# Four experts instead of two kept on chip at the end of a routed mixture of experts

## The chip, the cores and the metric

The kernel runs on one core of a Trainium2 chip. Five engines work side by side, each on its own list of instructions in order: PE (TensorE, matmul), DVE (VectorE), ACT (ScalarE), POOL (GpSimd) and SP (SyncE, which here only issues transfers). They wait for each other by semaphores. The metric is the time of one execution on the device in microseconds, as the median of several runs. All arithmetic is float32.

## What is computed

One hybrid decoder layer over 1024 tokens of width 1024: sparse attention beside a gated MLP, then a mixture of 32 experts, of which each token uses two, then a norm. The change touches the experts and what stands behind them:

```python
eid = g_idx * EXPERTS_PER_GROUP + e_idx
comb = jnp.sum(jax.nn.one_hot(eid, N_EXPERTS, dtype=jnp.float32) * e_w[..., None], axis=1).astype(h.dtype)
y = jnp.zeros_like(h)
for e in range(N_EXPERTS):
    he = jax.nn.silu(h @ w_gate[e]) * (h @ w_up[e])
    y = y + comb[:, e:e + 1] * (he @ w_down[e])
return y
...
x = x + y.reshape(B, T, D)
return rms_norm(x, final_norm_g)
```

`w_gate` and `w_up` are 1024x256 for each expert, `w_down` is 256x1024: 3 MB per expert, 100 MB in all.

## The kernel before

**Places.** The first six of the 32 places in the program take experts 0 to 5. A run sorts the others by how many tokens chose them, and each further place takes the expert of a certain rank (`ranks`). Behind the first six most odd places (`SMALLS`) are *small*: at most 64 tokens, up to 64 rows of a tile. Places 20, 24 and 28 (`PAIRS`) hold the fullest experts: such a place is two units, a first one of 128 rows (20a) and a second of up to 64 rows (20b) with the same weights. There are 35 units.

**A unit.** POOL gathers the rows of its tokens from DRAM (L1470), PE turns them (`xt`, L1486 or L1497), and PE multiplies by gate and up weights (`gu`). For a unit of 64 rows ACT puts the product aside (`junk`, L1543), PE turns it (`gut`, L1546), and ACT and DVE form silu(gate) x up (`kb`). PE then multiplies by the down weights (`y`), ACT evicts the result to `y` (L1513 for a small, L1591 for others), times each token's weight, and POOL adds its rows into the DRAM tensor `acc` with an indirect transfer (`scatter`, L1603). `acc` holds the layer's `x` to begin with. Two scatters could hit the same row, so each waits until the one before has landed. The results lie in a ring of three pages: an eviction waits until the scatter three before it has landed.

**Weights.** SP issues them in the order of `sequence`, into pages from a common pool, ahead of their use. A small uses them as float32 (one matmul counts as two passes). For the others ACT (`wh`, L132) and DVE (`wl`, L140) split each piece in two parts, and three matmuls (L145 to L147) take the place of one. With `EARLIER = 1` the gate and up weights of place 31 come ahead of the down weights of 29.

**The last two places**, 30 and 31, are small but are not scattered: their weighted results stay in `yh` and `yl` (high and low part, 64 rows each, `down` with `keep`; split weights). `spread` makes `S`, a table of zeros and ones that says to which token each kept row belongs.

**The end** (`finish`): SP reads `acc` back as eight tiles `xf` of 128 tokens (L1759). For each tile PE places the kept rows by `S` (four matmuls into `fin`, L1793); DVE adds `xf` (or PE does so for tiles 4 and 6, by a product with the identity, L1791). Square, root and reciprocal follow, the product with `final_norm_g` (`fg`, loaded by POOL at L1755), and the store (L1774). Four small lists (`lst`, `lsr`, `lsw`, `eod`) go to DRAM for a loop over overflow blocks that these inputs do not enter.

The order in each engine's list is set by a scheduler that places instructions by an estimate of times; `issue_after` ties an instruction to another one.

Of the kernel before, what the change touches and what calls it, by code (L numbers as in the profile page):

```python
# [21 lines left out]
P = 128  # L22
# [14 lines left out]
PAIRS = (20, 24, 28)  # L37
SMALLS = (9, 11, 13, 15, 17, 19, 21, 23, 25, 27, 29, 30, 31)
# [6 lines left out]
def ranks():  # L45

    n = NE - FIXED
    small = list(range(n - len(SMALLS), n))
    common = [e for e in range(FIXED, NE) if e not in PAIRS + SMALLS]
    return dict(zip(list(PAIRS) + common + list(SMALLS[-2:]) + list(SMALLS[:-2]), range(n)))  # L50

# [38 lines left out]
class Kern:  # L90
# [64 lines left out]
    def plan(self):  # L155
# [48 lines left out]
        for what, u in self.sequence():  # L204
            e, z = self.units[u]
            if z == 0 and what == "gu":
                gu(gets[e], None if e in SMALLS else "a")
            elif z == 0:
                dn(gets[e], (None, None) if e in SMALLS and e < NE - 2 else "aa")
# [19 lines left out]
    EARLIER = 1  # L229
# [1285 lines left out]

    def gate_up(self, x, r, piece):
# [33 lines left out]
        else:  # L1550
            a = nc.scalar.activation(sg, pp[:, :256], AF.Silu, scale=r)
            b = nc.vector.scalar_tensor_tensor(sg, pp[:, 256:], r, sg, op0=ALU.mult, op1=ALU.mult)
        self.hurry("g", a.ins, b.ins)
        return sg

    def down(self, wslot, sg, piece, keep=None):
# [13 lines left out]
        last = keep == HALF  # L1570
        if last and self.WARM:
            with self.tc.issue_after(self.lastsplit[0]):
                nc.scalar.activation(self.small([P, 1], F32, "warm", bufs=1), self.eps, AF.Sqrt)
        fs = [None, None]
        for f, c in ((0, 0), (1, 0), (0, 1), (1, 1)) if keep in self.COLS else ((0, 0), (0, 1), (1, 0), (1, 1)):
            fs[f] = fs[f] or piece()
            h, l = fs[f]
            cs = slice(c * 512, (c + 1) * 512)
            self.mm3(yp[:, c, :], hh[:, f, :], hl[:, f, :], h[:, cs], l[:, cs], f == 0, f == 1)
        y2 = yp.rearrange("p a b -> p (a b)")  # L1580
        if keep is not None:
            for c in range(self.KC):
                cs = slice(c * D // self.KC, (c + 1) * D // self.KC)
                h, l = (t[keep : keep + m, cs] for t in self.kept[1])
                nc.scalar.activation(h, y2[:, cs], AF.Copy, scale=wslot)
                nc.vector.scalar_tensor_tensor(l, y2[:, cs], wslot, h.bitcast(F32), op0=ALU.mult, op1=ALU.subtract)
            return None
# [28 lines left out]
    def moe(self):  # L1616
# [5 lines left out]
        def lists(u):  # L1622
# [4 lines left out]
            if e in SMALLS:  # L1627
                if e < NE - 2:
                    return self.tokp[: LIMITS[e], e : e + 1], self.rsd[:, e : e + 1], self.wsd[:, e : e + 1]
                return self.tokp[: LIMITS[e], e : e + 1], self.rsd[:, e : e + 1], self.wsp[:HALF, e : e + 1]  # L1630
# [28 lines left out]
        rows, ys = [], []  # L1659
        ovf = self.route_overflow()  # L1660
        for step in range(n + 2):
# [19 lines left out]
            while seq and seq[0][1] < step - (seq[0][0] == "dn") and seq[0][1] in (X if seq[0][0] == "gu" else G):  # L1681
# [5 lines left out]
                if units[u][0] in SMALLS and u < n - 2:  # L1687
                    e = units[u][0]
                    ys.append((self.tokh[:, e : e + 1], self.down_small(ws, G.pop(u), pieces(u, what))))
                    while len(ys) > (self.LATE if u < n - 3 else 0):  # L1690
                        self.scatter(*ys.pop(0))
                    continue
                if u == n - self.SPREAD:
                    self.kept = self.spread((NE - 2, NE - 1))
                if u >= n - 2:
                    self.down(ws, G.pop(u), pieces(u, what), keep=(u - n + 2) * HALF)
                else:
                    ys.append((tok, self.down(ws, G.pop(u), pieces(u, what))))
                while len(ys) > (self.LATE if u < n - 3 else 0):
                    self.scatter(*ys.pop(0))  # L1700
# [8 lines left out]
        with tc.issue_after(self.lastload.ins):  # L1709
# [34 lines left out]
    FIN_POOL = (0, 2)  # L1744
    FG, SPREAD = 1, 4
    WARM, COLS, KC = 1, (64,), 1
# [3 lines left out]

    def finish(self):

        nc, I = self.nc, self.I
        fg = self.page([P, D], F32, "fg")
        (nc.gpsimd if self.FG else nc.sync).dma_start(fg, I["final_norm_g"].rearrange("(o d) -> o d", o=1).to_broadcast([P, D]))  # L1755
        xs = []
        for i in range(8):
            x = self.page([P, D], F32, "xf")
            nc.sync.dma_start(x, self.acc[i * P : (i + 1) * P, :])  # L1759
            xs.append(x)  # L1760
        A = self.FIN_AHEAD
        for i in range(8 + A):
            if i < 8:
                self.finish_add(i, xs)
            if i >= A:
                j = i - A
                x, ss = xs[j]
                jk = self.page([P, D], F32, "fj")
                if j in self.FIN_POOL:
                    nc.scalar.activation(jk, x, AF.Copy, scale=ss)  # L1770
                    nc.gpsimd.tensor_tensor(jk, jk, fg, ALU.mult)
                else:
                    nc.vector.scalar_tensor_tensor(jk, x, ss, fg, op0=ALU.mult, op1=ALU.mult)  # L1773
                (nc.sync, nc.scalar)[j % 2 if self.FIN_Q else 0].dma_start(self.out[0][j * P : (j + 1) * P, :], jk)  # L1774

    FIN_AHEAD, FIN_Q, FIN_PE = 1, 0, (4, 6)

    def finish_add(self, i, xs):

        nc = self.nc  # L1780
        x = xs[i]
        if i % 2 and self.FIN_PS:
            pc = [self.ps1([P, 512], "fin", tag=t) for t in "ab"]
        else:
            ps = self.ps2("fin")
            pc = [ps[:, c, :] for c in range(2)]
        pe = i in self.FIN_PE
        for c in range(2):
            cs = slice(c * 512, (c + 1) * 512)
            if pe:  # L1790
# [38 lines left out]
```

## Time and profile before

| | us |
|---|---|
| median of three runs | 1225.43 (1221.41 to 1227.04) |
| the profiled execution | 1223.43 |
| its span (first to last instruction) | 1221.5 |
| PE busy | 1119.8 |
| DVE busy | 850.3 |
| ACT busy | 557.0 |
| POOL busy | 318.4 |

All times inside the profile are counted from the start of the span. The mean granted TensorE clock is 0.966 of full speed. PE is busy in 92% of the span, yet not at its end: in the page's last twentieth PE is busy in 3 to 6 tenths only, and no engine is busy in the last 12 us, where the last stores land. Three views carry the argument: the chain of waits that ended last, each engine's own timeline from 1100 us on, and windows of a few us that show which engines, and how much of the DMA, were busy in each stage. In a timeline the bracket behind an instruction says how long its engine stood idle before it, and what ended that.

### The profile page before, as it was taken

To read this page: it belongs to the slowest core of one execution; us is meant where nothing else is said; L and a number is where in the kernel's file an instruction comes from. 1 tells how busy PE (TensorE), PEld (TensorE's weight loads), DVE (VectorE), ACT (ScalarE), POOL (GpSimd) and SP (SyncE) were. 2 spreads that over 40 slices of the span, in tenths; PEclk is the share of its full clock that TensorE was granted. 3 is DMA by queue.
4 is the path that set the end of the run, shared out by engine and by line. 5 is a ranking of instruction groups with operands and counts; after the bars stand their busy time and mean duration, and the time that the engine had idled before them with its cause. 6 is when DMAs were issued, how large, how long until landed. Compare 5 with 4: busy or idle time off the path is not lost. (4 is left out here: it accounts for less than half of the span.)

```text
span 1221.5 us, 17405 instructions
## 1 busy us (share of the span) xinstructions
PE 1119.8 (92%) x5850; PEld 886.8 (73%) x5850; DVE 850.3 (70%) x1656; ACT 557.0 (46%) x992; POOL 318.4 (26%) x350
## 2 busy tenths in 40 slices
PE   4999999998999998899999989987999989999863
PEld 3789888887888886689987878865776555656431
DVE  7534889899999997588887951376897545345225
ACT  6424651312222212578775431324896455455324
POOL 5100033340021120044341542122243612223221
PEclk9999999998999998999999999997999979999986
DMA  7301021312422220000006755786999999999735
GB/s 224 87 18 35 18 72 33 99 40 69 121 86 87 86 86 18 18 1 1 2 2 207 249 191 180 256 291 211 306 313 309 305 333 335 335 335 335 229 88 231
DMA packets 148925, 190.68 MB, mean 156 GB/s; under 512 B 16994, under 2 KB 119946, under 8 KB 148834
## 3 DMA queue, kind: packets, MB, share of 16 engines
q1 hardware_dynamic: 134226, 156.85, 39.4%
q0 software_dynamic: 9568, 21.16, 7.0%
q10 hardware_dynamic: 5040, 11.54, 2.5%
q8 instruction: 47, 0.77, 0.3%
q14 instruction: 44, 0.36, 0.1%
HBM read 164.61 MB, written 33.74 MB: 162 GB/s over the span
## 5 line engine op out<-in xcount | busy, mean ns | idle before, releaser
L140 DVE TENSOR_TENSOR wl<-wr,wh 128x1024 fp32r<-128x1024 f32 x166 | 208.5, 1275 | 79.8 <-ACT wh L132 57.2
L132 ACT ACTIVATE wh<-wr 128x1024 fp32r<-128x1024 f32 x160 | 164.5, 1055 | 60.7 <-PE pj L146 28.5
L550 DVE TENSOR_SCALAR_CACHE_REDUCE junk<-idx,cand 128x384 bf16<-128x384 f32 (+2 forms) x198 | 186.9, 944 | 6.8 <-POOL idx L513 1.0
L145 PE MATMUL pj<-hT,wh 128*128 128x512 f32 (+1 forms) x464 | 179.8, 387 | 2.3 <-ACT wh L132 2.3
L147 PE MATMUL pj<-hT,wl 128*128 128x512 f32 (+1 forms) x464 | 178.5, 385 | 0.0
L146 PE MATMUL pj<-hT,wh 128*128 128x512 f32 (+1 forms) x464 | 178.2, 384 | 0.0
L145 PEld LDWEIGHTS pj<-hT,wh 128*128 128x128 f32 x464 | 87.9, 189 | 19.7 <-ACT wh L132 2.5
L147 PEld LDWEIGHTS pj<-hT,wl 128*128 128x128 f32 x464 | 87.8, 189 | 17.0
L146 PEld LDWEIGHTS pj<-hT,wh 128*128 128x128 f32 x464 | 87.8, 189 | 16.7
L890 POOL TENSOR_SCALAR P<-P,pair 128x128 f32<-128x128 f32 (+3 forms) x64 | 47.9, 748 | 88.3 <-DVE pair L889 80.0
L723 ACT ACTIVATE sb<-pj 128x512 f32<-128x512 f32 x32 | 19.0, 593 | 100.4 <-PE pj L147 100.4
L715 POOL TENSOR_TENSOR yt<-yt,sb 128x1024 f32<-128x1024 f32 x8 | 20.1, 2509 | 169.4 <-ACT sb L723 169.4
L145 PE MATMUL gu<-wh,xh 128*128 128x512 f32 x152 | 62.3, 410 | 1.2 <-ACT xh L132 0.8
L146 PE MATMUL gu<-wl,xh 128*128 128x512 f32 x152 | 63.0, 415 | 0.4
L147 PE MATMUL gu<-wh,xl 128*128 128x512 f32 x152 | 61.5, 404 | 0.0
L888 ACT ACTIVATE P<-S,pair 128x128 f32<-128x128 f32 (+3 forms) x64 | 47.4, 741 | 15.4 <-DVE pair L889 6.8
L510 DVE SCALAR_TENSOR_TENSOR idx<-rl,era,idx 128x384 f32<-128x384 f32 (+5 forms) x42 | 39.8, 947 | 20.1 <-ACT rl L506 18.9
L506 ACT ACTIVATE rl<-ix 128x384 f32<-128x384 f32 (+5 forms) x48 | 35.7, 760 | 38.9 <-PE ix L501 34.9
L145 PE MATMUL xo<-wh,m 128*128 128x512 f32 x128 | 51.4, 401 | 2.1 <-ACT m L132 1.7
L140 DVE TENSOR_TENSOR pt<-pt,pt 128x128 fp32r<-128x128 f32 (+2 forms) x96 | 50.6, 548 | 2.5 <-ACT pt L132 1.8
L147 PE MATMUL xo<-wh,m 128*128 128x512 f32 x128 | 50.2, 392 | 1.0 <-DVE m L140 1.0
L146 PE MATMUL xo<-wl,m 128*128 128x512 f32 x128 | 50.7, 396 | 0.0
(447 smaller groups left out, 2700.6 us busy)
## 6 DMA issues: line engine op xcount, KB each, us to landing
wr<-w_gate SPq DMA_DIRECT2D x128, 256.0 KB
wr<-w_up SPq DMA_DIRECT2D x128, 256.0 KB
wr<-w_down SPq DMA_DIRECT2D x64, 512.0 KB
wr<-w_in SPq DMA_DIRECT2D x33, 512.0 KB
x<-x SPq DMA_DIRECT2D x8, 512.0 KB
sga<-sb ACTq DMA_DIRECT2D x8, 512.0 KB
ybg<-yt POOLq DMA_DIRECT2D x8, 512.0 KB, 3.3
ybr<-ybg SPq DMA_DIRECT2D x8, 512.0 KB
```

The lines of the kernel that those rows point to most:

```text
L132: return nc.scalar.activation(out, src, AF.Copy)
L140: b = (self.nc.gpsimd if eng in "pq" else self.nc.vector).tensor_tensor(l, src, h.bitcast(F32), ALU.subtract)
L145: nc.tensor.matmul(out, lhsT=sh, rhs=mh, start=start, stop=False)
L146: nc.tensor.matmul(out, lhsT=sh, rhs=ml, start=False, stop=False)
L147: self.lastmm = nc.tensor.matmul(out, lhsT=sl, rhs=mh, start=False, stop=stop)
L506: nc.scalar.activation(r3, ps[:, :nch, :w], AF.Relu)
L510: nc.vector.scalar_tensor_tensor(acc, rl, wv, acc, op0=ALU.mult, op1=ALU.add)
L550: nc.vector.tensor_scalar(junk[:, : (j + 3) * P], self.idx[j + 2][:, : (j + 3) * P], cf[:, j : j + 1], None, op0=op, op1=ALU.add, accum_ou ...
L715: nc.gpsimd.tensor_tensor(yt, yt, sb, ALU.mult)
L723: self.nc.scalar.activation(sb[:, c * 512 : (c + 1) * 512], ps, AF.Sigmoid)
L888: nc.scalar.activation(p.rearrange("p (c w) -> p c w", c=nch), ps[:, :nch, :w], AF.Exp, bias=mx, scale=-1.0, accum_out=sm[:, 0:1])
L890: nc.gpsimd.tensor_scalar(p, p, sm[:, 1:2], 0.0, op0=ALU.mult, op1=ALU.add)
```

## The change

- `KEPT = 4`: places 28 to 31 are small and stay on chip, as two pairs (28 with 29, 30 with 31). `PAIRS` moves to 18, 22, 26; there are still 35 units, and 31 scatters for 33. `EARLIER` is 0.
- `down_pair` multiplies the two experts of a pair by their down weights as loaded, without splits: eight float32 matmuls into one PSUM tile (rows 0 to 63 and 64 to 127), then per 512 columns ACT evicts `yh` and DVE `yl`.
- Two tables `S`, two pairs of `yh` and `yl`, and `fg` (seven pages) are set aside at the down product of place 27, and `fg` is loaded there.
- In `finish` the rows of the first kept pair are placed by `finish_first`, up to three tiles ahead; `finish_add` adds the second pair and, for tiles 4 and 6, the identity product last.
- The four list writes are tied to the last read of `xf` rather than to the last weight. The warm-up of the root's table is tied to the last silu.

```diff
-PAIRS = (20, 24, 28)
-SMALLS = (9, 11, 13, 15, 17, 19, 21, 23, 25, 27, 29, 30, 31)
+PAIRS = (18, 22, 26)
+SMALLS = (9, 11, 13, 15, 17, 19, 21, 23, 25, 28, 29, 30, 31)
+
+KEPT = 4
...
-    EARLIER = 1
+    EARLIER = 0
...
+    def down_pair(self, pair, y):
+
+        nc = self.nc
+        w = self.pair()[:, 0:1]
+        for z, (e, _, _) in enumerate(pair):
+            r = slice(z * HALF, (z + 1) * HALF)
+            nc.vector.tensor_copy(w[r], self.wsd[r, e : e + 1])
+        yp = self.ps2("y")
+        for f in range(2):
+            for c in range(2):
+                for z, (_, sg, ws) in enumerate(pair):
+                    nc.tensor.matmul(yp[z * HALF : (z + 1) * HALF, c, :], lhsT=sg[:, f, :], rhs=ws[f][:, c * 512 : (c + 1) * 512], start=(f == 0), stop=(f == 1))
+        if pair[1][0] == NE - 1:
+            with self.tc.issue_after(self.lastsilu.ins):
+                nc.scalar.activation(self.small([P, 1], F32, "warm", bufs=1), self.eps, AF.Sqrt)
+        for c in range(2):
+            h, l = (t[:, c * 512 : (c + 1) * 512] for t in y)
+            nc.scalar.activation(h, yp[:, c, :], AF.Copy, scale=w)
+            nc.vector.scalar_tensor_tensor(l, yp[:, c, :], w, h.bitcast(F32), op0=ALU.mult, op1=ALU.subtract)
...
+                if u == n - KEPT - 1:
+                    self.kept = [self.spread((e, e + 1)) for e in range(NE - KEPT, NE, 2)]
+                    self.fg = self.page([P, D], F32, "fg")
+                    nc.gpsimd.dma_start(self.fg, I["final_norm_g"].rearrange("(o d) -> o d", o=1).to_broadcast([P, D]))
+                if u >= n - KEPT:
+                    pair.append((units[u][0], G.pop(u), [self.take() for _ in range(2)]))
+                    if len(pair) == 2:
+                        self.down_pair(pair, self.kept[(u - (n - KEPT)) // 2][1])
+                        pair = []
                     continue
...
-        with tc.issue_after(self.lastload.ins):
+        with tc.issue_after(self.lastread.ins):
             nc.sync.dma_start(lst, self.tok2)
...
+            while len(ps) < min(8, i + 1 + self.FIN_AHEAD):
+                ps.append(self.finish_first(len(ps)))
             if i < 8:
-                self.finish_add(i, xs)
-            if i >= A:
-                j = i - A
+                self.finish_add(i, xs, ps[i])
...
+    def kept_rows(self, pc, i, n, start, stop):
+
+        S, y = self.kept[n]
+        for c in range(2):
+            for z in range(2):
+                self.nc.tensor.matmul(pc[c], lhsT=S[:, i, :], rhs=y[z][:, c * 512 : (c + 1) * 512], start=(start and z == 0), stop=(stop and z == 1))
+
...
+        self.kept_rows(pc, i, 0, True, False)
...
+        for n in range(1, len(self.kept)):
+            self.kept_rows(pc, i, n, False, not pe and n == len(self.kept) - 1)
+        for c in range(2 if pe else 0):
+            nc.tensor.matmul(pc[c], lhsT=self.ident, rhs=x[:, c * 512 : (c + 1) * 512], start=False, stop=True)
```

How this stands in the engines' lists, at three places. First POOL, from a late gather to the last scatter, before. `acc<-` is a scatter: with `tokh` of a small, with `tok` of a pair's second half, with `tokp` of a unit of up to 128 rows; `h` or `g<-h2d` is a gather. The rows are the scatters of 23 and 24a, 24b, 25, 26, 27, 28a, 28b, then `fg`, then 29:

```order
L1470 DMA h_1127_6549<-h2d,tokp 64x1024
L1603 DMA acc<-y_7839,tokh 2048x512
L1603 DMA acc<-y_7840,tokp 1024x1024
L1603 DMA acc<-y_7841,tok_9240 1024x1024
L1603 DMA acc<-y_7839,tokh 2048x512
L1603 DMA acc<-y_7840,tokp 1024x1024
L1603 DMA acc<-y_7841,tokh 2048x512
L1603 DMA acc<-y_7839,tokp 1024x1024
L1603 DMA acc<-y_7840,tok_9240 1024x1024
L1755 DMA fg_10742<-final_norm_g 128x1024
L1603 DMA acc<-y_7841,tokh 2048x512
```

And now: behind the last gather 22a, `fg`, 22b, 23, 24, 25, 26a, 26b, 27.

```order
L1614 DMA acc<-y_7840,tokh 2048x512
L1472 DMA h_1127_6549<-h2d,tokp 64x1024
L1614 DMA acc<-y_7841,tokp 1024x1024
L1699 DMA fg_10529<-final_norm_g 128x1024
L1614 DMA acc<-y_7839,tok_9240 1024x1024
L1614 DMA acc<-y_7840,tokh 2048x512
L1614 DMA acc<-y_7841,tokp 1024x1024
L1614 DMA acc<-y_7839,tokh 2048x512
L1614 DMA acc<-y_7840,tokp 1024x1024
L1614 DMA acc<-y_7841,tok_9240 1024x1024
L1614 DMA acc<-y_7839,tokp 1024x1024
```

The last gather stood behind the scatter of 22 and ahead of the last nine; now it stands behind that of 21 (the first row) and ahead of the last eight, with `fg` among the early ones of these.

Second ACT, from the `junk` of place 31 (the last gate and up product) to the kept rows, before:

```order
L1543 ACTIVATE junk<-gu_10655,era_6541 128x512
L132 ACTIVATE wh_10664<-wr_10638 128x1024
L132 ACTIVATE wh_10670<-wr_10642 128x1024
L132 ACTIVATE wh_10686<-wr_10656 128x1024
L132 ACTIVATE wh_10692<-wr_10660 128x1024
L1591 ACTIVATE y_7840<-y_10361,era_6541 128x1024
L1513 ACTIVATE y_7841<-y_10455,era_6541 128x512
L1591 ACTIVATE y_7839<-y_10519,era_6541 128x1024
```

And now:

```order
L1565 ACTIVATE junk<-gu_10675,era_6541 128x512
L1602 ACTIVATE y_7840<-y_10360,era_6541 128x1024
L1602 ACTIVATE y_7841<-y_10449,ws_9241 64x1024
L1570 ACTIVATE kb_10684<-gut_10686 128x128
L1532 ACT_TABLE_LOAD
L1532 ACTIVATE warm_10705<-eps 128x1
L1602 ACTIVATE y_7839<-y_10538,era_6541 128x1024
L1535 ACTIVATE yh_10520<-y_10662,pair_10659 128x512 x2
L1535 ACTIVATE yh_10527<-y_10696,pair_10693 128x512 x2
```

The four `wh` splits are gone from between the last `junk` and the first eviction (of 26 before, of 26a now), and all that is left to evict stands behind that `junk`.

Third PE in the finish, before: the last rows of the kept rows of block 7 (`fin_10865`, `fin_10866`), then block 4 (`fin_10819`), with its identity product first in each half:

```order
L1793 MATMUL fin_10865<-yh_10593,S_10589 128x512
L1793 MATMUL fin_10865<-yl_10594,S_10589 128x512
L1793 MATMUL fin_10866<-yh_10593,S_10589 128x512
L1793 MATMUL fin_10866<-yl_10594,S_10589 128x512
L1791 MATMUL fin_10819<-xf_10752,identr 128x512
L1793 MATMUL fin_10819<-yh_10593,S_10589 128x512
L1793 MATMUL fin_10819<-yl_10594,S_10589 128x512
```

And now the end of block 6 (`fin_10798`), the identity product of block 4 (`fin_10759`), and block 7 (`fin_10818`, `fin_10819`):

```order
L1790 MATMUL fin_10798<-yh_10527,S_10523 128x512
L1790 MATMUL fin_10798<-yl_10528,S_10523 128x512
L1812 MATMUL fin_10759<-xf_10719,identr 128x512 x2
L1790 MATMUL fin_10818<-yh_10520,S_10516 128x512
L1790 MATMUL fin_10818<-yl_10521,S_10516 128x512
L1790 MATMUL fin_10818<-yh_10527,S_10523 128x512
L1790 MATMUL fin_10818<-yl_10528,S_10523 128x512
L1790 MATMUL fin_10819<-yh_10520,S_10516 128x512
L1790 MATMUL fin_10819<-yl_10521,S_10516 128x512
L1790 MATMUL fin_10819<-yh_10527,S_10523 128x512
L1790 MATMUL fin_10819<-yl_10528,S_10523 128x512
```

Block 7 had four matmuls ahead of blocks 4 and 6; it now has eight, behind block 6 and behind the product that waits for the read of tile 4.

## Rows read from the trace of the kernel before

**Rows 1.** Chain that ended last: start, us, what; from the last scatters on.

```profile
1182.31 3.59 DMA acc<-y,tokh
...
1189.33 10.29 DMA xf<-acc
...
1207.75 1.28 DVE fj L1773
```

**Rows 2.** Timeline of SP: start, us, queue, line, transfer, count; the reads.

```profile
1186.03 3.70 SPq L1759 DMA_DIRECT2D xf<-acc  x8
```

**Rows 3.** Waits on SP from 1100 us: total, times, longest us.

```profile
SPq L1759 <- DMA acc<-y,tokh: 41.3, 1, 41.3
...
SPq L194 <- PE gut L1546: 2.5, 1, 2.5
```

**Rows 4.** Timeline of POOL: start, us, transfer, [idle before, its releaser].

```profile
1123.39 2.27 POOL L1603 DMA_INDIRECT acc<-y,tokp  x1 [6.53 <-ACT wh L132]
1126.52 0.99 POOL L1470 DMA_INDIRECT h<-h2d,tokp  x1 [0.86 <-PE xt L1486]
1132.71 1.60 POOL L1603 DMA_INDIRECT acc<-y,tokh  x1 [5.20 <-DMA acc<-y,tokp]
1140.16 1.55 POOL L1603 DMA_INDIRECT acc<-y,tokp  x1 [5.85 <-DMA acc<-y,tokh]
1150.49 1.44 POOL L1603 DMA_INDIRECT acc<-y,tok  x1 [8.78 <-DMA acc<-y,tokp]
1154.58 1.55 POOL L1603 DMA_INDIRECT acc<-y,tokh  x1 [2.65 <-DMA acc<-y,tok]
1161.06 1.86 POOL L1603 DMA_INDIRECT acc<-y,tokp  x1 [4.93 <-ACT y L1591]
1167.07 1.55 POOL L1603 DMA_INDIRECT acc<-y,tokh  x1 [4.16 <-ACT y L1591]
1171.52 1.55 POOL L1603 DMA_INDIRECT acc<-y,tokp  x1 [2.89 <-ACT warm L1573]
1178.39 1.43 POOL L1603 DMA_INDIRECT acc<-y,tok  x1 [5.32 <-issue]
...
1182.31 1.60 POOL L1603 DMA_INDIRECT acc<-y,tokh  x1 [1.83 <-DMA acc<-y,tok]
```

**Rows 5.** Windows: length, busy us of each engine, PEclk, DMA share, GB/s.

```profile
1140.00:1150.00 10.00, 9.79 (x64) 5.05 (x64) 1.01 (x3) 3.92 (x8) 1.55 (x1) 1.00 1.02 342
1150.00:1155.00 5.00, 5.00 (x28) 2.02 (x24) 0.00 (x0) 0.31 (x1) 1.86 (x2) 1.00 0.16 36
...
1190.00:1195.00 5.00, 2.07 (x4) 1.16 (x4) 3.64 (x6) 4.08 (x8) 0.72 (x1) 0.50 0.99 376
```

**Rows 6.** Timeline of ACT: the eviction of 24b and the four splits.

```profile
1131.99 1.12 ACT L1591 ACTIVATE y<-y,ws 64x1024 f32<-64x1024 f32 x1 [1.50 <-DMA acc<-y,tokp]
...
1155.90 3.88 ACT L132 ACTIVATE wh<-wr 128x1024 fp32r<-128x1024 f32 x4
```

**Rows 7.** Timeline of PE at the end (a small's `gu` and `y` count passes).

```profile
1145.21 3.65 PE L1527 MATMUL gu<-wr,xs 128*64 128x512 f32 x16
...
1156.05 1.10 PE L1546 MATMUL gut<-ii,junk 128*128 128x64 f32 x8 [0.85 <-ACT junk L1543]
1160.84 0.80 PE L145 MATMUL y<-wh,kb 128*128 128x512 f32 x1 [3.68 <-ACT y L1591]
1161.43 0.63 PE L146 MATMUL y<-wl,kb 128*128 128x512 f32 x1
...
1164.42 0.63 PE L147 MATMUL y<-wh,kb 128*128 128x512 f32 x1
...
1168.52 1.94 PE L1509 MATMUL y<-wr,kb 128*64 128x512 f32 x8
...
1191.39 0.79 PE L1793 MATMUL fin<-yh,S 128*128 128x512 f32 x1 [9.89 <-DVE xf L1799]
```

**Rows 8.** Timeline of DVE: the first tile's sum, and that of tile 7.

```profile
1189.38 1.22 DVE L1805 TENSOR_TENSOR xf<-fin,xf 128x1024 f32<-128x1024 f32 x1 [10.77 <-DMA xf<-acc]
...
1199.71 1.29 DVE L1799 TENSOR_TENSOR xf<-fin,xf 128x512 f32<-128x512 f32 x2 [0.66 <-DMA xf<-acc]
```

## What I predict

> **What bounds the kernel now.** I read the chain of waits first, from its end [rows 1]: the last arithmetic ends at 1209.03 us of the span (1207.75 plus 1.28); before it lie the eight reads of `acc` (10.29 us from the last issue to the last landing), and before those the landing of the scatter of expert 29, issued at 1182.31 and landed 3.59 later. So the end hangs on the moment R at which the last scatter has landed and SP may issue the reads: R = 1186.03 us [rows 2], after SP had stood still for 41.3 us [rows 3].
>
> The POOL timeline tells why R is so late [rows 4]. Every scatter adds into `acc`, and each waits until the one before has landed. While the weights stream, one takes long: 22 to 23 is 9.32 us, 24a to 24b is 10.33, 23 to 24a is 7.45. The stream ends at 1150: DMA share 1.02 and 342 GB/s before, 0.16 and 36 GB/s after [rows 5]. From there the same scatters are short: 26 (80 rows) 6.01 until the next is issued, 27 (a small) 4.45, 28a (128 rows) 6.87, 28b (64 rows) 3.92, 29 (a small) 3.59. At 1150.49 scatter 24b is issued, the 27th of 33. Six stand behind it, and with it they take until 1186.
>
> Two more things stand on this tail. ACT splits four weight pieces at 1155.90 (3.88 us) ahead of the eviction of 26 [rows 6]. PE waits for that eviction 3.68 us and comes back at the lower of its two clock levels [rows 7]: starts lie 2.99/7 = 0.43 us apart, against 3.65/16 = 0.23 for a pass at the full clock. Scatter 26 is therefore issued at 1161.06, although 25, a small issued at 1154.58, must have landed near 1158.2 to 1159 (3.59 to 4.45 us): 2 to 3 us of the chain are lost there.
>
> **What the change does to that chain.** Two more experts stay on chip, so 31 scatters remain. Pairs now stand at 18, 22, 26, so the 27th scatter is that of expert 24, and behind it stand four: 25, 26a, 26b, 27. Up to the 27th the two programs scatter as many units and as many pairs (18 and 22 for 20 and 24); the order among them differs.
>
> When is the 27th issued? The order on POOL has the last gather, for expert 31, ahead of 22a; it waits for the transposes of expert 28. Before, the last gather stood behind 22 and went out at 1126.52 after a wait for such transposes of 0.86 us [rows 4]. PE is busy almost without a gap from there to the last gate and up product [rows 5], so the place of the transposes of 28 can be counted back from its end (1156.5, below): 8 passes of the product of 27, four small products of 3.65, the downs of 25, 26a and 26b (1.94 and two of 2.8), three transposes and four turns of a result (1.10, [rows 7]) are 30 us. That puts them near 1126.5 again. So 22a goes out near 1127.5, 4 us later than the 24th scatter before (22, at 1123.39). Then 128 loaded rows (10.33), 64 rows and a small at 7.45 each give 24 at 1152.7. If nothing is lost at the gather, the equal count gives 1150.5. The chip moves the same bytes in that time, apart from `fg`, whose 512 KB are 1.5 us at 342 GB/s and go out between 22a and 22b, where POOL waits in any case. I take 1151.7.
>
> From there nothing streams: 24 as 26 before (6.01), 25 as 29 (3.59; as 27, 4.45), 26a 6.87, 26b 3.92, 27 6.01, in all 26.4 to 27.3. So R = 1151.7 + 26.6 = 1178.3, between 1176.9 and 1180.0, against 1186.03: **7.7 us earlier** (6 to 9).
>
> Are the five results ready? ACT evicts in order, and each eviction into the ring of three waits for the landing three scatters earlier (before: 1.50 us in front of the eviction of 24b, [rows 6]). 26a now waits for 23 (landed near 1152) and for the last activation of the stream (about 1157.5, below), so it is evicted by 1158.7; 26b waits for 24 (1157.7), 27 for 25 (1161.3). They are scattered from 1161.3, 1168.2 and 1172.1: 2 to 9 us to spare. Without the four splits nothing else is in front. A 24 evicted late would only hold the `xs` of the experts behind it, whose products run after 1144.
>
> PE until the stream ends: the pair's earlier place and raw weights change its work by about +1 us, so the last gate and up product ends near 1156.5 against 1155.2. Behind it PE has 28 matmuls for 52: 12 for expert 27 and, per pair of experts, 8 of two passes (a small's 4 such matmuls take 1.94 us, [rows 7]), so 2.8 + 3.7 + 3.7 = 10.2 us at the full clock, 19 at the lower. The first kept pair is on chip near 1166.5, the second near 1170.5 (two ACT evictions of about 0.7 and two of DVE behind each). Then 32 placing matmuls for blocks 0 to 3 against 16 before: 7.4 us, done near 1178, or 1184 at the lower clock. The first read lands 3.35 us after R (1189.38, [rows 8]), so this is hidden or costs up to 2.
>
> **The reads and the finish.** Eight reads of the same size land in the same 13.6 us, since they are bound by DMA (share 0.99, [rows 5]). After them the new price: placing the kept rows of blocks 4 to 7 takes 32 matmuls for 16, that is 16 x 0.23 = 3.7 us to 16 x 0.43 = 6.9. Most of it fits between the landings: before, PE waited 9.89 us ahead of the first of these and worked in 2.07 of the 5 us from 1190 [rows 5, 7]. The block that ends the chain is 7. Before, its sum was ready at 1197.5 and DVE added x7 when the read had landed, 1199.71 = R + 13.7 [rows 8]. In the order of after, block 7 stands behind blocks 5, 4, 6 and the identity product of 4. Block 6 needs the bank that x2 frees (R + 8.6), so it ends at R + 10.5 to 12; the identity product of 4 then ends by R + 14, block 7 by R + 14.5 to 16. So x7 comes 0.8 to 2.3 us later, partly covered since DVE is full from there with other blocks' products. I take **+0.7** (0 to +4, the upper end if little of the 6.9 fits between the landings).
>
> The four small list writes go behind the reads on SP, where the next entry is an output that waits for its block: nothing. They were at 1141 before, out of the chain. The table load for the root moves ahead of the last evictions (1.28 us of ACT before, where it also preceded an eviction): nothing. From the last block to the end of the execution 12.4 us remain as they are (1221.5 - 1209.1).
>
> Sum: 1223.43 (this execution) - 7.7 + 0.7 = 1216.4. The three runs before had a median of 1225.43, 2.0 above the profiled execution, so against that scale **1218.4**.
>
> **A rule that speaks for more.** Unloaded, the scatter of 128 rows took 6.87 us and that of 64 rows 3.92 [rows 4]. The Trainium skill, in "DMA: Bandwidth & Descriptors", section "Anatomy of one DMA — SWDGE (gpsimd) path", fits such a transfer by 2.0 us plus bytes over 436e3; as an estimate by that page 512 KB would take 3.2 us and 256 KB 2.6, the five scatters some 14 us for 26.6, and the time would be near 1206. This trace disagrees by half; the rule has 0.02 of rival (b), which holds whatever makes the scatters quicker than their rows.
>
> **Rivals.** (a) *The gain is eaten on PE.* The kept rows cost what the scatters saved. For it: PE is at the lower clock in the first 10 us of the reads (granted 0.50 in 1190 to 1195, [rows 5]), and R now comes sooner after the placing products. If blocks 0 to 3 end at 1184 and all 16 added matmuls run at 0.43, the finish is 4 to 7 us longer: 1225.4 - 7.7 + 6 = 1223.7, within 1221 to 1226. Against it: PE has slack between the landings. Chance 0.22.
>
> (b) *More than that.* The gather holds up nothing and the loaded scatters take 7.45 rather than 10.33: 22a at 1123.4, 24 at 1146, R at 1173, some 13 us earlier: 1213. For it: the spread of the loaded times. The unloaded five may be quicker than their rows, too. Against it: the last gather had been waited for. That the reads no longer wait for scatters at all I exclude: `acc` is one tensor, and the first read needs the landing of 27 in the order as well. Chance 0.12.
>
> (c) *Slower.* The last gather now stands ahead of the last eight scatters, in front of the pair's 22a; on its transposes PE works behind activations, those behind ring evictions, and these behind scatters. If the transposes of 28 come D late, all eight move by D. Two weight units late (6 MB, 18.4 us at 342 GB/s) gives 1225.4 - 7 + 18.4 = 1237; it costs from D = 7 and shows as slower from D = 13. Seven pages set aside two units before the kept ones leave the stream fewer pages, which could start it. For it: SP stood waiting for PE in this stretch too (2.5 us in front of one piece, [rows 3]). Against it: before, that gather waited 0.86 us only. Chance 0.08.
>
> (d) *The change does nothing to the end* (a last scatter late for an unseen reason, reads at 1186 as before, finish +1): 1226. It is counted with (a).
>
> **How the numbers follow.** The forecast, 1216 to 1222, has 0.58. A measurement of this kernel tells about 0.5% from no change, 6.1 us, that is below 1219.3; the forecast lies 0.9 us inside, and of its 0.58 I put 0.39 below the line. With (b) that is 0.51 faster. Same: 0.19 of the forecast and 0.18 of (a), 0.37. Slower: 0.04 of (a) and (c), 0.12. The range 1211 to 1227 takes in the bounds of R and the finish and (a), and most of (b); it leaves out (c), the worst of (a) and the best of (b), under 2 in 10.
>
> **What would show it.** Right: 31 scatters, the 27th issued at 1150 to 1153, the last five in 26 to 28 us without an ACT eviction as releaser, the first `xf` read near 1178 and the last `fj` some 23 to 25 us later. Wrong in the first step: a gather or 22a after 1130, or the stream's end after 1153. Wrong in the second: gaps of POOL behind ACT among the last five. Wrong in the third: x7 added later than R + 16, with PE busy at the lower clock in front of it.

## The result

| | before | after |
|---|---|---|
| first comparison, six runs each: median | 1226.24 us | 1212.24 us |
| ratio, 95% interval | | 0.9897 (0.9868 to 0.9926) |
| second comparison (19 and 6 runs): median | 1223.87 us | 1213.05 us |
| ratio, 95% interval | | 0.9905 (0.9884 to 0.9927) |
| the profiled execution, its span | 1223.43, 1221.5 | 1216.06, 1214.3 |

The change makes the kernel 11 to 14 us faster, about 1%. Forecast were 7 us on the profiled execution and 1218 for the median. The two profiled executions lie 7.4 us apart, so the forecast fits these and is 5 to 6 us short of the medians; where the rest comes from is the first thing the experiments had to tell. The medians lie below the band of 1216 to 1222, which had a chance of 0.58. They lie inside the wide range of 1211 to 1227 because that took in rival (b), 1213, which had 0.12.

POOL of the kernel after, the columns as in [rows 4]; 21, the last gather, 22a, `fg`, 22b, 23, 24, 25, 26a, 26b, 27:

```profile
1114.66 2.08 POOL L1614 DMA_INDIRECT acc<-y,tokh  x1 [1.43 <-ACT wh L134]
1124.15 0.96 POOL L1472 DMA_INDIRECT h<-h2d,tokp  x1 [7.41 <-PE xt L1499]
1125.42 1.57 POOL L1614 DMA_INDIRECT acc<-y,tokp  x1 [0.30 <-issue]
1126.45 1.20 POOL L1699 DMA_DIRECT2D fg<-final_norm_g  x1
1137.29 1.49 POOL L1614 DMA_INDIRECT acc<-y,tok  x1 [9.65 <-DMA acc<-y,tokp]
1144.33 1.57 POOL L1614 DMA_INDIRECT acc<-y,tokh  x1 [5.54 <-DMA acc<-y,tok]
1151.83 1.45 POOL L1614 DMA_INDIRECT acc<-y,tokp  x1 [5.92 <-DMA acc<-y,tokh]
1160.01 1.57 POOL L1614 DMA_INDIRECT acc<-y,tokh  x1 [6.74 <-issue]
1164.42 1.56 POOL L1614 DMA_INDIRECT acc<-y,tokp  x1 [2.84 <-DMA acc<-y,tokh]
1171.15 1.42 POOL L1614 DMA_INDIRECT acc<-y,tok  x1 [5.17 <-ACT yh L1535]
1175.31 1.42 POOL L1614 DMA_INDIRECT acc<-y,tokp  x1 [2.73 <-PE fin L1790]
```

SP's reads, as in [rows 2], and the chain of waits that ended last (start, us, what), from the last scatters on:

```profile
1180.11 3.75 SPq L1767 DMA_DIRECT2D xf<-acc  x8
```

```profile
1160.01 3.68 DMA acc<-y,tokh
...
1163.77 1.12 ACT y L1602
...
1175.31 4.75 DMA acc<-y,tokp
...
1185.49 7.24 PE fin L1790 x24
1192.73 1.72 PE fin L1812 x4
1194.45 1.86 PE fin L1790 x8
1196.31 1.73 PE fin L1812 x4
...
1201.93 1.24 DVE fj L1782
```

R, the issue of the first read, is 1180.11 against 1186.03; the 27th scatter (24) went out at 1151.83. The chain looks as it did up to the reads. Behind them it now runs over PE and not over the landing of the reads, as in [rows 1].

PE at the same place as [rows 7]: it goes from the last turned result to the down product of 27 without a stop, at full pace (12 matmuls from 1157.09 to 1160.15), and is done with the placing of blocks 0 to 3 at 1176.15.

```profile
1156.09 1.10 PE L1568 MATMUL gut<-ii,junk 128*128 128x64 f32 x8 [0.85 <-ACT junk L1565]
1157.09 0.50 PE L147 MATMUL y<-wh,kb 128*128 128x512 f32 x1
...
1160.47 3.65 PE L1529 MATMUL y<-wr,kb 128*64 128x512 f32 x16 [0.31 <-ACT y L1602]
1164.93 3.72 PE L1529 MATMUL y<-wr,kb 128*64 128x512 f32 x16 [0.81 <-ACT y L1602]
...
1175.54 0.61 PE L1790 MATMUL fin<-yl,S 128*128 128x512 f32 x2
1185.49 0.79 PE L1790 MATMUL fin<-yh,S 128*128 128x512 f32 x1 [9.34 <-DVE xf L1818]
```

Windows, as in [rows 5]: the stream of weights now ends some 5 us later (1.04 and 398 GB/s where 0.16 and 36 stood), and the granted clock stays at 1.00 from 1160 to 1165, where it was 0.50 before.

```profile
1150.00:1155.00 5.00, 5.00 (x28) 2.34 (x26) 0.58 (x2) 0.55 (x2) 1.45 (x1) 1.00 1.04 398
1155.00:1160.00 5.00, 4.15 (x22) 3.14 (x20) 0.00 (x0) 2.38 (x3) 0.00 (x0) 1.00 0.41 108
1160.00:1165.00 5.00, 3.88 (x18) 1.13 (x18) 0.29 (x1) 3.30 (x6) 2.15 (x2) 1.00 0.06 5
```

And DVE, as in [rows 8]: the first sum, and the sum of tile 7 in two halves, each of which waits for PE.

```profile
1184.75 0.69 DVE L1818 TENSOR_TENSOR xf<-fin,xf 128x512 f32<-128x512 f32 x1 [13.07 <-DMA xf<-acc]
...
1195.42 0.69 DVE L1818 TENSOR_TENSOR xf<-fin,xf 128x512 f32<-128x512 f32 x1 [0.70 <-PE fin L1790]
1196.35 0.69 DVE L1818 TENSOR_TENSOR xf<-fin,xf 128x512 f32<-128x512 f32 x1 [0.24 <-PE fin L1790]
```

### The profile page after: what moved, and what is told of

Its sections match the earlier page's. It is cut to its first block, busy times and chain, and to the rows that moved or that the text cites. A ratio compares the mean times of both kernels' runs of the same rounds, so it can differ in the third digit from the quotient of the medians.

```text
span 1214.3 us, 17426 instructions
## 1 busy us (share of the span) xinstructions
PE 1118.9 (92%) x5874; PEld 890.2 (73%) x5874; DVE 852.2 (70%) x1659; ACT 552.6 (46%) x986; POOL 318.6 (26%) x348
## 5 line engine op out<-in xcount | busy, mean ns | idle before, releaser
L142 DVE TENSOR_TENSOR wl<-wr,wh 128x1024 fp32r<-128x1024 f32 x162 | 203.6, 1275 | 58.8 <-ACT wh L134 46.5
L134 ACT ACTIVATE wh<-wr 128x1024 fp32r<-128x1024 f32 x156 | 160.8, 1055 | 65.7 <-PE pj L148 28.5
L890 ACT ACTIVATE P<-S,pair 128x128 f32<-128x128 f32 (+3 forms) x64 | 47.4, 741 | 15.3 <-DVE pair L891 6.8
```

What stands on the lines that cost most here:

```text
L134: return nc.scalar.activation(out, src, AF.Copy)
L142: b = (self.nc.gpsimd if eng in "pq" else self.nc.vector).tensor_tensor(l, src, h.bitcast(F32), ALU.subtract)
L890: nc.scalar.activation(p.rearrange("p (c w) -> p c w", c=nch), ps[:, :nch, :w], AF.Exp, bias=mx, scale=-1.0, accum_out=sm[:, 0:1])
```

## The experiments

### Both kernels again

No edit. A second trace of each was to tell whether 7 or 11 to 14 us are the change's work, and in which stage.

> The kernel before once more, for a second trace. Both theories expect a ratio of 1.00 within 0.3%. Question: in the first pair of traces the profiled executions lie 7.4 us apart (1223.43 and 1216.06), the medians 14.0. If the gain is all in the tail (theory 1), the distance from the issue of the first expert's scatter to the last sum of rows is the same in both traces of this kernel within 2 us, and what differs lies ahead of the experts. If the tail itself varies between executions (theory 2), that distance differs by 4 us or more.

> The changed kernel once more. Theory 1 (the gain is the scatter chain, some 7 to 8 us, and the first trace of this kernel fell on an execution that lost time before the experts): 1211 to 1214 us, and in the trace the reads start near 1175, with 24 issued near 1147 and five scatters of 26 to 28 us behind it. Theory 2 (the tail varies): reads again near 1180 and a time near 1216.

Measured: 1223.42 (ratio 0.9996, 0.9981 to 1.001) and 1213.05. The reads started at 1186.06 and at 1177.29 (expected near 1175), and 24 went out at 1150.91 (expected near 1147). The scatters of 24 and 25 in the second trace of the changed kernel:

```profile
1150.91 1.45 POOL L1614 DMA_INDIRECT acc<-y,tokp  x1 [6.00 <-ACT kb L1570]
1157.10 1.57 POOL L1614 DMA_INDIRECT acc<-y,tokh  x1 [4.75 <-issue]
```

So theory 1 holds in part: the first trace of the changed kernel had lost 3 us before its first expert. Its first scatter stands at 865.92, in the second trace at 863.08, in the kernel before at 862.79 and 861.79. One loss can be seen: from 200 to 300 us, long ahead of the change, PE worked 89.94 us in that execution, 95.65 in that of before, in stages whose work is the same (the first row is of before, the second of after).

```profile
200.00:300.00 100.00, 95.65 (x450) 80.35 (x449) 94.18 (x189) 23.44 (x30) 24.29 (x24) 0.97 0.22 69
```

```profile
200.00:300.00 100.00, 89.94 (x428) 75.41 (x427) 94.97 (x178) 22.73 (x29) 24.55 (x24) 0.95 0.21 63
```

Times within the span are therefore compared between traces from two marks: the first scatter, and the last `gut` product (the product of the last gate and up weights is done then; the start of `gut` counts). In us:

| trace | first scatter to last `gut` | `gut` to R | R to end of last `fj` | from there to the end of the span |
|---|---|---|---|---|
| before | 293.3 | 30.0 | 23.0 | 12.5 |
| before, again | 294.0 | 30.2 | 21.9 | 13.5 |
| after | 290.2 | 24.0 | 23.1 | 11.1 |
| after, again | 291.6 | 22.6 | 24.5 | 10.7 |
| e3: two kept | 293.4 | 28.7 | 21.8 | 11.3 |
| e7: before, raw pair | 293.6 | 28.0 | 23.5 | 11.9 |
| e4: no scatter of 27 | 289.2 | 19.6 | 23.5 | 11.5 |
| e8: none of 26, 27 | 292.1 | 6.2 | 28.2 | 10.5 |
| e5: pages late | 290.3 | 22.1 | 23.8 | 10.9 |
| e9: gather behind 22a | 294.7 | 22.1 | 23.3 | 11.7 |
| e10: e5 and e9 | 292.5 | 21.8 | 24.2 | 13.0 |
| e11: lists, `fg` back | 289.4 | 23.2 | 25.1 | 12.6 |
| e12: one pair placed | 288.5 | 23.7 | 21.9 | 11.2 |

From the last `gut` to the end of the span it is 65.5 us before (mean of two) and 58.0 after: the tail gives **7.5 us**. Another 2.7 (293.65 against 290.9) come ahead of it. Counted from the first scatter, R stands at 314.2 in both traces of the changed kernel and at 323.2 and 324.3 before. Each version but these two has one trace, and versions that do the same work in a stage differ there by 2 us, in the first column by 6, so smaller differences in this table show nothing by themselves.

### One part alone: the pair with raw weights, and the new code with two kept

e7 is the kernel before with one edit: its two kept experts go through `down_pair`, with weights as loaded. e3 is the changed kernel with two kept experts at the old places:

```diff
-PAIRS = (18, 22, 26)
-SMALLS = (9, 11, 13, 15, 17, 19, 21, 23, 25, 28, 29, 30, 31)
-KEPT = 4
+PAIRS = (20, 24, 28)
+SMALLS = (9, 11, 13, 15, 17, 19, 21, 23, 25, 27, 29, 30, 31)
+KEPT = 2
...
-    EARLIER = 0
+    EARLIER = 1
...
```

> The kernel before with one part of the change alone: the two kept experts as one pair with weights as loaded, no splits. Finish, lists and final_norm_g as before. Run e3 (this plus the new finish, lists and final_norm_g) was 4.8 us below before. Theory (the four splits delay the eviction of 26 and PE's return): 2 to 4 us faster than before, 1220 to 1222. Rival (the 4.8 are the new finish): 1223 to 1224.

> The new code with two experts kept instead of four, pairs at 20, 24, 28 as before and 33 scatters: it has the raw kept pair, the new finish and the early final_norm_g, but not the two scatters less. Theory 1 (the scatters behind the last weights are the price): 2 to 3 us faster than before, 1222 to 1224, since the four splits of the last evictions are gone, and 7 to 9 us slower than the changed kernel. Rival (the gain is the splits and the shorter work of PE at the end): most of the gain is there already, 1212 to 1217.

Measured: e7 1222.25 (0.999, 0.9979 to 1.0002), e3 1219.09 (0.9963, 0.9945 to 0.9981). In the trace of e7 the splits are gone and scatter 26 follows the landing of 25; PE no longer stops. ACT, then POOL from 25 to 27:

```profile
1156.23 0.69 ACT L1563 ACTIVATE junk<-gu,era 128x512 f32<-128x512 f32 x1 [4.37 <-PE gu L1547]
1156.82 1.11 ACT L1612 ACTIVATE y<-y,era 128x1024 f32<-128x1024 f32 x1
```

```profile
1155.66 1.55 POOL L1624 DMA_INDIRECT acc<-y,tokh  x1 [2.89 <-DMA acc<-y,tok]
1160.09 1.43 POOL L1624 DMA_INDIRECT acc<-y,tokp  x1 [2.88 <-issue]
1165.94 1.55 POOL L1624 DMA_INDIRECT acc<-y,tokh  x1 [4.42 <-DMA acc<-y,tokp]
```

25 to 26 is 4.43 us, for 6.48 in [rows 4]: 2.1 us, which is what `gut` to R shows (28.0 for 30.1). The median moved by 0.7 only, with no gain and 2.6 us both within its interval. e3, at 1219.09, lies between what theory 1 and the rival expected. In its trace `gut` to R is 1.4 us shorter than before, and R to the end some 2 us shorter than in both traces of before and in e7.

From e3 to the changed kernel two scatters fewer follow (with the pairs moved and `EARLIER` at 0, which no run tells apart). R comes 28.7 - 23.3 = 5.4 us sooner behind the last `gut`, but the whole tail shortens from 61.8 to 58.0 only, since the finish is longer. So of the 7.5 us of the tail e3 has 3.7 and the step to four kept 3.8. By the medians it is 4.8 (interval 2.3 to 6.7) and 6.0 us. At R the scatters have the larger part; at the end the rival (splits and PE's end, with the new finish) has about half.

### The chain alone: without 27, without 26 and 27

```diff
                     ys.append((tok, self.down(ws, G.pop(u), pieces(u, what))))
+                    if u == n - KEPT - 1:
+                        ys.pop()
```

(e8: `u >= n - KEPT - 3`.)

> The changed kernel without the last scatter: the rows of place 27 are computed and evicted but never added. Theory 1: the last scatter took 4.75 us from issue to landing in the first trace and nothing else is late, so the time is 4 to 5 us below the changed kernel (1207 to 1209). Rival (the finish is bound by PE, that places the kept rows, or the reads by something else): within 1.5 us of the changed kernel.

> The changed kernel without its last three scatters (26a, 26b, 27), whose rows are computed and evicted but not added. They took 6.8, 4.1 and 4.8 us. If only the chain decided: 15.5 us below the changed kernel, 1197 to 1198. Theory (PE is behind it with its first 32 placing matmuls, done near 1174): the reads start near 1162 and the finish waits for PE, so 4 to 8 us of it are lost: 1202 to 1206.

Measured: 1206.23 (ratio to before 0.9843, 0.9817 to 0.987) and 1199.47 (0.9806, 0.9788 to 0.9824). Without 27 the tail is 54.6 us long for 58.0, and the median is 6.8 below, a little more than expected; the two have the 4.8 of that scatter between them. Without three scatters R comes 17 us sooner after the last `gut`, and the end 13. The missing 4 are in the finish, where DVE's first sums now wait for PE, the first until 9 us behind R (4.6 in the changed kernel):

```profile
1168.53 0.69 DVE L1820 TENSOR_TENSOR xf<-fin,xf 128x512 f32<-128x512 f32 x1 [1.06 <-PE fin L1792]
1170.57 1.22 DVE L1824 TENSOR_TENSOR xf<-fin,xf 128x1024 f32<-128x1024 f32 x1 [1.35 <-PE fin L1792]
```

So the chain still decides the end of the changed kernel, and PE stands some 13 us behind it (an estimate from one trace, 17 less 4). The loss of 4 us is the lower end of what was expected; the time, 13.6 us below the changed kernel by the medians, lies below the expected 1202 to 1206 and above the 1197 to 1198 of the chain alone.

### Six experts kept

```diff
-PAIRS = (18, 22, 26)
-SMALLS = (9, 11, 13, 15, 17, 19, 21, 23, 25, 28, 29, 30, 31)
-KEPT = 4
+PAIRS = (16, 20, 24)
+SMALLS = (9, 11, 13, 15, 17, 19, 21, 26, 27, 28, 29, 30, 31)
+KEPT = 6
```

> Six experts kept (26 to 31, as three pairs), pairs of units at 16, 20, 24, so 29 scatters. If the chain alone decided, two scatters less are another 8 to 10 us: 1203 to 1205. Theory (behind the chain stands PE, some 6 us behind): three pairs' down products and 48 placing matmuls in front of the reads are 11 + 11 us behind the last gate and up product and 2.8 for the last eviction, so PE is ready near 1180 while the reads would land from 1172; most of it is lost: 1208 to 1213.

Measured: 1214.64 (0.9928, 0.9912 to 0.9943): no better than four, and above the expected 1208 to 1213. The reads start at 1161.72, 10 us sooner than expected, but the first sum comes 21 us later, behind PE, which works without a gap (5.00 of 5 us from 1160 to 1195). DVE, then windows:

```profile
1182.72 1.23 DVE L1822 TENSOR_TENSOR xf<-fin,xf 128x1024 f32<-128x1024 f32 x1 [1.57 <-PE fin L1790]
```

```profile
1175.00:1180.00 5.00, 5.00 (x22) 2.35 (x19) 0.75 (x1) 1.01 (x2) 0.00 (x0) 1.00 0.00 0
1180.00:1185.00 5.00, 5.00 (x22) 3.79 (x21) 3.03 (x4) 1.39 (x3) 0.00 (x0) 1.00 0.00 0
```

The last `gut` is at 1171.65 here, 16 to 17 us later than with four kept, which the expectation had not seen. PE places rows of the first pair before it (the second row is one of several such):

```profile
1166.51 1.94 PE L1549 MATMUL gu<-wr,xs 128*64 128x512 f32 x8
1169.23 0.73 PE L1790 MATMUL fin<-yh,S 128*128 128x512 f32 x2
1171.65 1.00 PE L1568 MATMUL gut<-ii,junk 128*128 128x64 f32 x8
```

The trace shows that the bound has gone to PE, which is busy for 1129.7 us of the span, for 1118.9 and 1120.6 with four kept; how much of it the later products and how much the added placing make up is not told apart.

### Where the changed kernel still waits: pages, the gather, the lists

e5 sets the second pair's pages and `fg` aside at the first pair's down product:

```diff
-                    self.kept = [self.spread((e, e + 1)) for e in range(NE - KEPT, NE, 2)]
-                    self.fg = self.page([P, D], F32, "fg")
-                    nc.gpsimd.dma_start(self.fg, I["final_norm_g"].rearrange("(o d) -> o d", o=1).to_broadcast([P, D]))
+                    self.kept = [self.spread((NE - 4, NE - 3))]
...
+                        if len(self.kept) == 1:
+                            self.kept.append(self.spread((NE - 2, NE - 1)))
+                            self.fg = self.page([P, D], F32, "fg")
+                            nc.gpsimd.dma_start(self.fg, I["final_norm_g"].rearrange("(o d) -> o d", o=1).to_broadcast([P, D]))
```

> The changed kernel with only the first kept pair's three pages set aside at place 27; the second pair's three pages and final_norm_g follow at the first pair's down product. In the two traces of the changed kernel SP issued the last down weights 7 to 10 us later than before, the weight stream ended 3 to 7 us later, and scatter 24 took 8.18 and 6.19 us. Theory (the seven pages hold up the stream and with it the chain): the stream ends near 1151, scatter 24 takes 6 us, 1 to 2 us faster, 1211 to 1212. Rival (the stream's end has slack): 1213, no difference.

Measured: 1212.16 (0.9911, 0.9897 to 0.9925), no difference. The tail in its trace is 1.2 us shorter, and scatter 24 took 6.42 us, so the late stream can cost about what was expected, but the times do not show it.

e9 ties the gather of expert 31 to the scatter of 22a, so that it stands behind it on POOL; e10 is e5 and e9 in one:

```diff
+                with tc.issue_after(self.scats[23]) if u == n - 1 else nullcontext():
-                rows.append(self.gather(...))
+                    rows.append(self.gather(...))
```

> The changed kernel with one transfer moved: the gather of expert 31 stands behind the scatter of 22a on POOL instead of ahead of it. In both traces of the changed kernel POOL waited 7.41 us for the transposes of 28 in front of that gather, and 22a went out 10.8 us after the scatter of 21, where a loaded scatter of a small otherwise takes 7.5 to 8.3. Theory (the chain decides the end): 22a and all behind it 2 to 3 us earlier, R near 1175 and the time 2 to 3 us below the changed kernel. Rival (the gather hid behind the scatter): no difference.

> Run e9 and run e5 in one: the gather behind 22a, and the second pair's pages and final_norm_g set aside later. Run e5 alone was no faster than the changed kernel (1212.2). Theory: as e9, 2 to 3 us below the changed kernel, and up to 1 more since the stream ends sooner. Rival: as e9 or as e5, no more than the better of the two.

Measured: 1210.27 (0.9885, 0.987 to 0.9901) and 1209.96 (0.9878, 0.9858 to 0.9898): 2 to 3 us below the changed kernel by the medians and by the ratios of the second comparison (0.0020 and 0.0027 of 1224), as expected, with intervals that overlap its own. Of the versions that add all rows they are the fastest found; that they beat the changed kernel is possible, not shown. POOL of e9, the scatter of 21, 22a, and the gather behind it:

```profile
1116.97 1.91 POOL L1615 DMA_INDIRECT acc<-y,tokh  x1 [1.59 <-ACT wh L134]
1126.05 1.58 POOL L1615 DMA_INDIRECT acc<-y,tokp  x1 [7.17 <-DMA acc<-y,tokh]
1127.93 0.98 POOL L1472 DMA_INDIRECT h<-h2d,tokp  x1 [0.30 <-DMA wr<-w_up]
```

From 21 to 22a it is 9.08 us, for 10.76 in the first trace of the changed kernel: 1.7 us. The wait of 7.41 us in front of the gather lay mostly in the shadow of the landing of 21, which alone takes until 9 us behind its issue here (the expectation had 7.5 to 8.3). Not all of it reaches R, which comes 22.1 us (e10 21.8) after the last `gut` for 24.0 and 22.6: scatter 24 takes 8.44 us in e9. Both traces are of the slowest of five executions (1216.17 and 1214.96), R of e9 stands at 1179.48 rather than near 1175, and the tails, 57.0 and 59.0 us, lie around the 58.0 of the changed kernel, so the traces do not show the gain of the medians.

e11 puts the list writes ahead of the reads again, and moves the lines that set `fg` aside and load it into the finish (the diff shows the first):

```diff
-        with tc.issue_after(self.lastread.ins):
+        with tc.issue_after(self.lastload.ins):
```

> The changed kernel with its two small moves undone: the four list writes ahead of the reads again, and final_norm_g set aside and loaded in the finish, on POOL behind the last scatter. Theory (both were hidden before and after): no difference from the changed kernel, within 1.5 us. Rival (the later final_norm_g frees a page and 1.5 us of the stream, or the lists hold SP): 2 us either way.

Measured: 1213.92 (0.992, 0.9907 to 0.9934): 0.9 us above the changed kernel by the medians and 1.8 by the ratios of the second comparison, with intervals that overlap. That shows no difference, but neither does it decide between the theory's 1.5 us and the rival's 2: in its one trace the tail is 60.9 us long for 58.0, with 25.1 from R to the last `fj`.

### The price of placing

```diff
-        self.kept_rows(pc, i, 0, True, False)
+        self.kept_rows(pc, i, 0, True, i not in self.FIN_PE)
...
-        for n in range(1, len(self.kept)):
-            self.kept_rows(pc, i, n, False, not pe and n == len(self.kept) - 1)
```

> The changed kernel without placing the rows of the second kept pair: 32 of the 64 placing matmuls are left out, 16 of them behind the reads; the rows are computed and kept but not added. Theory (the placing hides between the landings but for block 7, whose sum came 0.8 to 2.3 us late): 1 to 2 us below the changed kernel. Rival (PE bounds the finish): 4 us or more below. If nothing: the finish has slack for it all.

Measured: 1209.76 (0.9894, 0.9874 to 0.9914), 3.3 us below the changed kernel by the medians and 1.3 by the ratios of the second comparison; the intervals overlap, so the times alone show no gain. In the trace R to the last `fj` is 21.9 us for 23.1 and 24.5, and the sum of tile 7 waits for nothing (1185.90, R + 14.3; in the changed kernel R + 15.3 and R + 16.7). So the placing costs the finish 1 to 2.5 us by the traces, not 4.

## Why the prediction was right, and where its size was off

The change came out faster, and the steps that were named gave what they were to give at R, the moment of the first read, within 2 us; the size was 7 for 11 to 14 us. The term that was mis-sized is the stage up to the last gate and up product: it was put 1.3 us later than before (1156.5 for 1155.2) and came 2.7 us sooner, counted from the first scatter, on the average of the traces.

**The issue of the 27th scatter** was put at 1151.7 and stood at 1151.83 and 1150.91. Three errors cancelled there. POOL waited 7.41 us for the transposes in front of the last gather, not 0.86, but 22a went out at 1125.42, before 1127.5; the scatters up to 24 then took 26.4 us, not 25.2; and the first trace was 3 us late from its first scatter on. Counted from there the 27th stands at 285.9 and 287.8 us, for 287.7 and 288.1 before, and was put at 288.9.

**The last five** were to take 26.6 us and took 28.3 and 26.4. Scatter 24 was taken as unloaded. In the first trace the stream still ran (398 GB/s up to 1155, 108 behind it) and it took 8.18; 6.19 in the second. The stream's end after 1153, named as a sign that the first step is wrong, so came true in the first trace, and it cost about 2 us there. 27 landed 4.8 and 5.0 us after its issue, not 6.01. None of the five waited long for its result: the ACT eviction named in front of 26b is of kept rows, and its own result was on chip at 1160.42, 10.7 us earlier.

**R** was to come 7.7 us earlier and came 5.9 and 8.8 us earlier by the span, 6.8 (30.1 to 23.3) from the last `gut`. e7 and e3 show its two parts: 1.4 to 2.1 us from the splits in front of the eviction of 26, and the other 4.7 to 5.4 from the two scatters.

**The finish** was to grow by 0.7 and grew by 1.3 up to the last `fj` (mean of two traces each), by the named way: block 7 is ready at R + 15.3 and 16.7, put at 14.5 to 16. The second lies past R + 16, the sign that the third step is wrong, but PE was not at the lower clock in front of it (granted 1.00 from 1190 to 1195, ahead of the sum at 1194.00). From the last `fj` to the end of the span it took 2.1 us less (13.0 to 10.9), where the prediction had the 12.4 us "as they are". That this is the change's work is not shown: the four traces with two kept experts have 11.3 to 13.5 us there, the nine with four 10.5 to 13.0. Over the whole finish, from R to the end, before has 35.5 and 35.3 us and the changed kernel 34.2 and 35.2.

**The rest of the gain** has two sources. The first is the scale. The step "2.0 above the profiled execution" took the median of three runs for the kernel's. Over the six runs of the first comparison it is 1226.24, 2.8 above the profiled execution, and over the 19 of the second 1223.87, 0.4 above; by the latter the forecast is 1216.8 and not 1218.4. So it is mainly the medians of before that make the gain 14.0 us in one comparison and 10.8 in the other; the traces, from the first scatter to the end of the span, have 10.3 (359.2 to 348.9). The second is a stage in which the prediction saw no change but fg's 1.5 us and PE's 1 us, as costs: from the first scatter to the last `gut` it takes 293.3 to 294.0 us in all four traces with two kept experts, and 288.5 to 294.7 in nine with four, 290.9 on average. Part of it is seen at one place. Near 985 us PE waits for ACT to split `kb`, the turned product that goes into a down product. In ACT's list that split stands behind one of a weight piece (`wh`), and ACT waits for this piece to land. First ACT and PE before, then after:

```profile
984.00 1.06 ACT L132 ACTIVATE wh<-wr 128x1024 fp32r<-128x1024 f32 x1 [2.66 <-DMA wr<-w_up]
985.55 0.80 PE L145 MATMUL y<-wh,kb 128*128 128x512 f32 x1 [3.60 <-ACT kb L132]
```

```profile
984.43 1.06 ACT L134 ACTIVATE wh<-wr 128x1024 fp32r<-128x1024 f32 x1 [0.20 <-DMA wr<-w_up]
985.98 0.80 PE L147 MATMUL y<-wh,kb 128*128 128x512 f32 x1 [0.73 <-ACT kb L134]
```

PE's wait is 3.3 to 3.7 us in the four traces with two kept, and with four kept 0.7 to 1.6 in five (after, e4, e5, e11, e12) and 3.1 to 3.4 in four (after again, e8, e9, e10). ACT's wait for the piece is 0.2 to 0.4 us in the five and 2.4 to 2.9 in the other eight. The five have the shorter stage, 288.5 to 290.3 against 291.6 to 294.7. Why the piece lands in time in some executions of the same program, and how much of the 2.7 us the change earns, stays open.

**The rivals.** (a), the gain eaten on PE, did not come: PE ran at the full clock from 1157 to 1176 and was done 4 us before R. e12 shows its price (1 to 2.5 us), e6 and e8 where it would begin: by the estimate from e8, with R some 13 us ahead of that of the changed kernel. (b), more than that, was right in its size by luck and wrong in its way: R came 6 and 9 us earlier for its 13, and the scatters were as slow as forecast. (c), the slow loop over the last gather, did not come: the gather went out 2 us sooner than before, and e9 puts its price at 1.7 us at most. The rule of the Trainium skill ("DMA: Bandwidth & Descriptors", section "Anatomy of one DMA — SWDGE (gpsimd) path"), by which 3.2 and 2.6 us were estimated, was not borne out: the 128 rows took 6.73 and 6.80 us in the two traces, the 64 rows 4.16 and 4.09.

## What to carry to other kernels

Where transfers that add into one tensor must follow one another, count how many are left when the stream beside them ends, and price these few unloaded: that count gave the gain at R, behind the last product, within 1 us. Each result taken out of such a chain moves work to the engine that puts it back, so look how far behind the chain that engine stands before taking out more; here two cost the finish 1 to 2.5 us and the next two brought nothing. Compare traces from marks near the change, and set a forecast against many runs, since executions of one program lose 3 us and more in stages that no edit touched.

## What the runs showed that was not expected

- A wait can be long and cost little: 7.41 us of POOL in front of the last gather were worth at most 1.7 us of the chain (e9), as the scatter behind it had to wait for a landing anyway.
- DVE's product with `fg`, 1.28 us by itself, took 2.70 beside POOL's product in e11 and 3.01 in e10, as it took 2.80 and 3.04 in the two traces of before; in the two traces of the changed kernel the products of both engines overlap by at most 0.3 us, and it took 1.28 each time. POOL and DVE of e11:

```profile
1189.34 2.35 POOL L1780 TENSOR_TENSOR fj<-fj,fg 128x1024 f32<-128x1024 f32 x1 [1.23 <-ACT fj L1779]
1190.08 2.70 DVE L1782 SCALAR_TENSOR_TENSOR fj<-xf,pair,fg 128x1024 f32<-128x1024 f32 x1
1193.82 1.28 DVE L1782 SCALAR_TENSOR_TENSOR fj<-fin,pair,fg 128x1024 f32<-128x1024 f32 x1
```

- In the changed kernel PE goes on behind the last product without a gap of over 0.9 us, and the granted clock stays at 1.00 (1160 to 1165); before, it came back from the stop of 3.68 us at 0.50, for 4 us. With the splits gone alone (e7) it was 1.00 there too.
